# Hybrid gMLP/Mamba-2 trunk, passage to layer B: two subtractions, the time steps and a gate result moved, eight stores on another queue

## The chip, the cores and the metric

The kernel runs on one core of one Trainium2 chip. The metric is the device time of one execution in microseconds. The engines are TensorE (PE in the profile; PEld is its weight load), VectorE (DVE), ScalarE (ACT), GpSimd (POOL) and SyncE (SP), which only issues transfers. Each engine works through its own instructions in order and waits on semaphores for the others.

## The reference, cut to what matters

The trunk has two layers over 1024 tokens of width 1024. Layer A is a causal spatial gating mixer, layer B a Mamba-2 mixer. Each adds its output to the residual stream.

```python
def ssd_mixer(h, w_in, conv_w, conv_b, dt_bias, a_log, d_skip, norm_w, w_out):
    proj = h @ w_in                                   # 1024 x 1024 by 1024 x 6176
    z = proj[..., :D_INNER]                           # gate, 2048 columns
    xbc = proj[..., D_INNER:D_INNER + B_CONV_DIM]     # x, B and C, 4096 columns
    dt_raw = proj[..., D_INNER + B_CONV_DIM:]         # time steps, 32 columns
    xbc = jax.nn.silu(causal_depthwise_conv(xbc, conv_w, conv_b))
    dt = jax.nn.softplus(dt_raw + dt_bias)
    ...
    gated = (y * jax.nn.silu(z)) ...
for i in range(DEPTH):
    hn = rmsnorm(h, norm_w[i])
    h = h + mixer_i(hn)
```

What matters here is the start of layer B: `hn` is the normalised output of layer A, and the first thing computed from it is `z = hn @ w_in[:, :2048]`, with `silu(z)` kept for later, and the 32 time-step columns.

## The kernel before, in words

All large products are in float32 precision made of three passes: an operand is split into a high part (`wh`, `hh`: a cast, ScalarE, line 111) and a low part (`wl`, `hl`: source minus high part, VectorE, line 112), and `mm3` (lines 134 to 136) issues high by high, high by low and low by high. So each weight operand waits first for ScalarE and then for VectorE.

On top of this, each block of columns is computed by Strassen's scheme in Winograd's form: the activations and the weights are cut into halves both ways, and seven products replace eight. The activations' operands are `A11, A12, S4, A22, S1, S2, S3` for products 1 to 7 and are shared by all blocks; the weights' operands are `b[0,0]`, `b[1,0]`, the fourth sum (`fourth()`, line 225, `b21 - t2`), `t1`, `t2` and so on, per block. `Block.prep(n)` (line 242 on) splits the weights of product n, `Block.mm(n, i)` issues its 12 `mm3` for unit i (24 matmuls for a product of two units and 4 steps), and `Block.post(n, i)` takes a finished accumulator out of PSUM: products 1, 6 and 7 are copied to `u` by ScalarE (line 292); products 2, 5, 7 with 4, and 3 complete the quarters C11, C22, C21 and C12, and call the block's `done`. Products 6 and 7 add onto the accumulator of product 1, so product 7 must wait for the copies of product 6; product 3 adds onto that of product 5.

For the gate blocks (`z_block`, line 987 on) `done` adds the accumulator and `u` on VectorE into a tile `zt` (line 995), and `rest` applies SiLU on ScalarE (line 1000) and stores the 256 KB to `z_d` by ScalarE's queue (line 1001). The first gate block does this at once; later blocks put it off. `zt` shares a pool of four buffers (`k2`) with the time steps' `part` and the time-step weights. PSUM has six `acc` banks, three pairs of a product's two units, and two `sm` banks.

The passage from layer A to layer B is `into_b` (line 1047 on). It is written out by hand, in `manual_schedule`: each engine executes its instructions in the order in which the program names them. While the last product of layer A's output still runs, rows are normalised (`norm`, line 1059), transposed on TensorE (`tr`, line 1065) and split into operands (`first`, `second`; `both` is a cast and a subtraction, lines 1073 and 1077). `s3(tt)` (line 1103) and `s2_a(tt)` (line 1108) are VectorE subtractions that make the sums behind S3 and S2; `s2_b` splits S2 and, for every second `tt`, lets GpSimd issue an accumulating transfer for S4 (line 1114). `dt_mm(th)` computes the time steps of half the tokens into a `sm` bank, and `dt_post(th)` (lines 1037 to 1041) takes them out: a ScalarE copy, a VectorE addition, two ScalarE activations into `dtr`. The order of the first gate block is 1, 2, 4, 6, 7, 5, 3, and with the loads, `prep` and product 1 of the second block (`nxt`) behind it. `blocks` then runs the second gate block and the convolution blocks, with the decays of the time steps (`decays`, from line 1236) worked in between. The weights of the convolution blocks are summed by accumulating transfers that GpSimd issues (line 202).

Of the kernel before, what the change touches and what calls it, by code (L numbers as in the profile page):

```python
# [8 lines left out]
F32 = mybir.dt.float32  # L9
F32R = mybir.dt.float32r  # L10
AF = mybir.ActivationFunctionType
ALU = mybir.AluOpType
# [17 lines left out]
def kernel(  # L30
# [21 lines left out]
    nc = tc.nc  # L52
    x = x[0]
    out = out[0]
# [10 lines left out]
    def s8(shape, name, dt=F32):  # L65
        return sb.tile(shape, dt, name=name, tag="s8", bufs=16)
# [4 lines left out]
    def k2(shape, name, dt=F32):  # L71
        return sb.tile(shape, dt, name=name, tag="k2", bufs=4)
# [10 lines left out]
    def wh(shape):  # L83
        return sb.tile(shape, F32R, name="wh", tag="wh", bufs=3)

    def wl(shape):
        return sb.tile(shape, F32R, name="wl", tag="wl", bufs=3)
# [9 lines left out]
    def sm(name):  # L97
        return ps[0].tile([P, 512], F32, name=name, tag="sm", bufs=n_sm[0])
# [7 lines left out]
    def split(hi, lo, src, eng=None, sign=1.0):  # L106

        if sign < 0:
            nc.scalar.mul(hi, src, sign)
            return nc.vector.scalar_tensor_tensor(lo, src, sign, hi.bitcast(F32), ALU.mult, ALU.subtract)  # L110
        nc.scalar.copy(out=hi, in_=src)  # L111
        return (eng or nc.vector).tensor_tensor(out=lo, in0=src, in1=hi.bitcast(F32), op=ALU.subtract)  # L112
# [69 lines left out]
    class Block:  # L182
# [56 lines left out]
                TT(out=self.t1, in0=b[0, 1], in1=b[0, 0], op=ALU.subtract)  # L239
                TT(out=self.t2, in0=b[1, 1], in1=self.t1, op=ALU.subtract)  # L240

        def prep(self, n, lo=None):
            b = self.b
            if self.eng is not None:
                self.sum_up(n)
            src = {1: b[0, 0], 2: b[1, 0], 4: b[1, 0], 7: b[0, 1], 3: b[1, 1]}.get(n)
            if src is None:
                src = self.t1 if n == 5 else self.t2
            h_, l_ = wh([P, 4, self.cols]), wl([P, 4, self.cols])
            split(h_, l_, src, lo)  # L250
            self.Y[n] = (h_, l_)

        def sum_up(self, n):
            b, TT = self.b, self.eng.tensor_tensor
            if n in (4, 6):
                self.sums()
            if n == 4 and not self.t4:
                self.fourth()
            if n == 7:
                TT(out=b[0, 1], in0=b[1, 1], in1=b[0, 1], op=ALU.subtract)  # L260
# [291 lines left out]
    for gp in range(G // 2):  # L552
# [4 lines left out]
        if gp == 1:  # L557
# [9 lines left out]
            for h in range(2):  # L567
# [9 lines left out]
                for k in range(4):  # L577
                    g = h * 4 + k
# [25 lines left out]
    for g in range(G):  # L604
# [26 lines left out]
        def mix(m, th):  # L631
            c = g * 2 + m
            mx = sm("mx")
            for q in range(4):
# [11 lines left out]
        blk = Block(HS, lambda kh, j: [a_w_in[kh * 512:(kh + 1) * 512, j * DI + g * 256:j * DI + (g + 1) * 256]],  # L646
                    False, done_zu)
# [330 lines left out]
    z_d = [dr.tile([P, 2, T], F32, name=f"z_d{g}") for g in range(G)]  # L978
# [3 lines left out]
    def finish():  # L982

        while late:
            late.pop(0)()

    def z_block(b):

        wide = 256 if b < 3 else 128

        def done(name, i, a, u):
            th, j = 2 - int(name[1]), int(name[2]) - 1
            zt = k2([P, 512], "zt")
            if u is not None:
                nc.vector.tensor_tensor(out=zt, in0=a, in1=u, op=ALU.add)
                a = zt
            g, m = (2 * b + j, i) if b < 3 else (6, j)

            def rest():
                nc.scalar.activation(zt, a, AF.Silu)  # L1000
                nc.scalar.dma_start(out=z_d[g][:, m, th * 512:(th + 1) * 512], in_=zt)

            late.append(rest)
            if not b:
                finish()

        def W(kh, j):
            c = 512 * b + j * wide
            return [b_w_in[kh * 512:(kh + 1) * 512, c:c + wide]]

        return Block(H2, W, False, done, None, wide)

    def dt_load():


        raw = wr([P, 8, 32])
        nc.sync.dma_start(out=raw, in_=b_w_in[:, c0:c0 + 32].rearrange("(k p) n -> p k n", p=P))
        w1 = k2([P, 8, 64], "wdt", F32R)
        split(w1[:, :, 0:32], w1[:, :, 32:64], raw)
        nc.vector.tensor_tensor(out=raw[:, 4:8], in0=raw[:, 4:8], in1=raw[:, 0:4], op=ALU.subtract)  # L1020
        w0 = sb.tile([P, 4, 64], F32R, name="wdt", tag="k1", bufs=3)
        split(w0[:, :, 0:32], w0[:, :, 32:64], raw[:, 4:8])
        return [w1[:, 0:4], w0], [w1[:, 0:4], w1[:, 4:8]]

    def dt_mm(th, w):
        pd = sm("pd")
        for kh in range(2):
            X = H2[(("S1", "A22"), ("A11", "A12"))[th][kh]]
            for k in range(4):
                for x_ in X:  # L1030
                    nc.tensor.matmul(out=pd[0:64, :], lhsT=w[th][kh][:, k, :], rhs=x_[:, k, :],
                                     start=kh + k == 0 and x_ is X[0], stop=kh + k == 4 and x_ is X[1])
        return pd

    def dt_post(th, pd):
        part = k2([32, 512], "part")
        nc.scalar.copy(out=part, in_=pd[32:64, :])
        nc.vector.tensor_tensor(out=part, in0=pd[0:32, :], in1=part, op=ALU.add)
        for j in range(2):
            q = th * 2 + j  # L1040
            nc.scalar.activation(dtr[q * 32:(q + 1) * 32, :], part[:, j * 256:(j + 1) * 256], AF.Identity,
                                 bias=hv[0:32, 0:1])
# [4 lines left out]
    def into_b():  # L1047
# [4 lines left out]
        blk = zb[0]  # L1052
# [47 lines left out]
        def s3(tt):  # L1100
            if tt == 0:
                st["s3"] = s8([P, 4, 4, P], "s3")
            TTv(out=st["s3"][:, tt], in0=F[1, tt][:, 0], in1=F[0, tt][:, 0], op=ALU.subtract)

        def s2_a(tt):

            f0 = F[1, tt][:, 0]
            TTv(out=f0, in0=f0, in1=F[0, tt][:, 1], op=ALU.subtract)
# [7 lines left out]
        def both(name, tt, src):  # L1116
            hi(name, tt, src)
            lo(name, tt, src)
# [8 lines left out]
        wdt = dt_load()  # L1127
# [39 lines left out]
        pd = dt_mm(1, wdt)  # L1167
# [7 lines left out]
        blk.eng = V  # L1175
        blk.fourth()
        blk.eng = None
        blk.prep(4)
        blk.post(1, 0), blk.post(1, 1)
        s2_a(0), s3(3), s2_a(1)  # L1180
        for i in range(2):
            blk.mm(2, i, False)
        s2_b(0), s2_a(2), s2_b(1), s2_a(3), s2_b(2), s2_b(3)
        blk.prep(6)
        for tt in range(4):
            both("S3", tt, st["s3"][:, tt])
        dt_post(1, pd)
        blk.prep(7)
        for i in range(2):
            blk.mm(4, i, False)  # L1190
        for i in range(2):
            blk.mm(6, i, False)
        blk.post(6, 0), blk.post(6, 1)
        blk.post(2, 0), blk.post(2, 1)
        for i in range(2):
            blk.mm(7, i, False)
        for tt in range(4):
# [3 lines left out]
            blk.post(7, i, (0,))  # L1201
        for i in range(2):
            blk.mm(5, i, False)
        pd = dt_mm(0, wdt)
        nxt = zb[1]
        for kh, j in ((0, 0), (1, 0), (0, 1), (1, 1)):
            nxt.load(kh, j)
# [2 lines left out]
        blk.prep(3)  # L1210
        blk.post(5, 0), blk.post(5, 1)
        nxt.prep(1)
        for i in range(2):
            blk.mm(3, i, False)
        for i in range(2):
            blk.post(7, i, (1,))
        nxt.prep(2)
        for i in range(2):
            nxt.mm(1, i, False)
        dt_post(0, pd)  # L1220
        nxt.sums()
        for i in range(2):
            blk.post(3, i), nxt.post(1, i)

# [155 lines left out]
    def projections():  # L1380
# [41 lines left out]
        for kh in range(2):  # L1422
            prep(0, kh)
            yield
        last = 0
        for i, (g, kind) in enumerate(seq):
            for m in range(2):
                drain(len(queue) - last)
                ab = acc2("ab")
                for kh in range(2):  # L1430
                    for th in (1, 0):
                        for k in range(4):
                            mm3(ab[:, th, :], [w[:, k, m * P:(m + 1) * P] for w in W[i, kh]],
                                [h_[:, k, :] for h_ in H2[f"A{2 - th}{kh + 1}"]], kh == 0 and k == 0,
                                kh == 1 and k == 3)
                            if (kh, th, k) == (1, 0, 3):
                                last = push(g, kind, m, ab)
                            if k % 2:
                                yield
                    if (m, kh) == (0, 1):  # L1440
                        prep(i + 1, 0)
                    elif (m, kh) == (1, 0):
                        prep(i + 1, 1)
# [74 lines left out]
    with tc.manual_schedule():  # L1518
        into_b()
        blocks()  # L1520
# [483 lines left out]
```

## Time and profile before

| | |
|---|---|
| median of 3 runs | 1522.73 us (1522.0 to 1526.09) |
| the profiled execution: its time | 1524.54 us |
| its span | 1522.8 us |
| granted TensorE clock | 0.995 |
| TensorE busy | 97% of the span |
| VectorE, ScalarE, GpSimd busy | 69%, 51%, 26% |
| the passage, from the first transpose to the second gate block's first product | 670 to 746 us |

A row of a timeline has the start in us from the span's start, the duration in us, the engine, the line of the kernel, the operation, the tile written and those read, the shapes and a count. In brackets stands the time that the engine stood idle before it, and what ended that. A row with a count above 1 stands for several instructions in sequence. Instructions of one engine overlap a little at their edges, so the distance of starts is the cost in a row of them: 0.227 us for a matmul of 512 columns, whatever its own 0.39.

### The profile page before, as it was taken

To read this page: it belongs to the slowest core of one execution; us is meant where nothing else is said; L and a number is where in the kernel's file an instruction comes from. 1 tells how busy PE (TensorE), PEld (TensorE's weight loads), DVE (VectorE), ACT (ScalarE), POOL (GpSimd) and SP (SyncE) were. 2 spreads that over 40 slices of the span, in tenths; PEclk is the share of its full clock that TensorE was granted. 3 is DMA by queue.
4 is the path that set the end of the run, shared out by engine and by line. 5 is a ranking of instruction groups with operands and counts; after the bars stand their busy time and mean duration, and the time that the engine had idled before them with its cause. 6 is when DMAs were issued, how large, how long until landed. Compare 5 with 4: busy or idle time off the path is not lost. (4 is left out here: it accounts for less than half of the span.)

```text
span 1522.8 us, 21294 instructions
## 1 busy us (share of the span) xinstructions
PE 1477.8 (97%) x7834; PEld 1219.0 (80%) x7834; DVE 1052.6 (69%) x1712; ACT 784.2 (51%) x1257; POOL 393.3 (26%) x435
## 2 busy tenths in 40 slices
PE   6899999999999999999999999999999999999997
PEld 6899988888888888877778888877777777777875
DVE  7956566676666645678646467867677677688876
ACT  6533332322332445556656566656676666756463
POOL 1111010000000023202021223207576766642221
PEclk9999999999999999999999999999999999999999
DMA  5554323332322999947277978687666665579972
GB/s 182 140 172 141 105 89 113 105 111 93 116 96 82 351 256 239 250 130 159 97 172 153 207 152 166 139 241 208 181 153 187 160 184 139 168 250 279 258 149 111
DMA packets 175976, 254.45 MB, mean 167 GB/s; under 512 B 16400, under 2 KB 103168, under 8 KB 172672
## 3 DMA queue, kind: packets, MB, share of 16 engines
q1 hardware_dynamic: 124768, 168.93, 36.2%
q0 software_dynamic: 41168, 66.07, 22.3%
q10 hardware_dynamic: 9936, 18.09, 3.3%
q8 instruction: 62, 1.02, 0.3%
q14 instruction: 42, 0.34, 0.1%
HBM read 186.14 MB, written 51.18 MB: 156 GB/s over the span
## 5 line engine op out<-in xcount | busy, mean ns | idle before, releaser
L134 PE MATMUL acc<-hh,wh 128*128 128x512 f32 x868 | 340.9, 393 | 3.0 <-ACT wh L111 2.2
L136 PE MATMUL acc<-hh,wl 128*128 128x512 f32 x868 | 339.1, 391 | 4.3 <-DVE wl L112 4.3
L135 PE MATMUL acc<-hl,wh 128*128 128x512 f32 x868 | 338.0, 389 | 0.0
L112 DVE TENSOR_TENSOR wl<-wr,wh 128x1024 fp32r<-128x1024 f32 (+1 forms) x97 | 115.5, 1193 | 127.7 <-ACT wh L111 127.6
L136 PEld LDWEIGHTS acc<-hh,wl 128*128 128x128 f32 x868 | 162.9, 188 | 42.2 <-DVE wl L112 8.4
L134 PEld LDWEIGHTS acc<-hh,wh 128*128 128x128 f32 x868 | 163.0, 188 | 39.2 <-ACT wh L111 4.3
L135 PEld LDWEIGHTS acc<-hl,wh 128*128 128x128 f32 x868 | 163.1, 188 | 32.9
L292 ACT COPY u<-acc 128x512 f32<-128x512 f32 x115 | 66.7, 582 | 193.4 <-PE acc L136 192.1
L111 ACT CAST wh<-wr 128x1024 fp32r<-128x1024 f32 (+1 forms) x113 | 116.3, 1030 | 95.4 <-PE acc L135 56.7
L136 PE MATMUL acc<-wh,hl 128*128 128x256 f32 x448 | 128.6, 287 | 4.9 <-DVE hl L403 3.5
L134 PE MATMUL acc<-wh,hh 128*128 128x256 f32 x448 | 129.0, 288 | 3.4 <-DVE wh L414 1.4
L134 PE MATMUL ab<-hh,wh 128*128 128x512 f32 x288 | 128.2, 445 | 2.1 <-DVE x L1305 1.1
L135 PE MATMUL acc<-wl,hh 128*128 128x256 f32 x448 | 128.1, 286 | 1.3 <-DVE wl L417 1.3
L136 PE MATMUL ab<-hh,wl 128*128 128x512 f32 x288 | 113.4, 394 | 0.0
L135 PE MATMUL ab<-hl,wh 128*128 128x512 f32 x288 | 112.3, 390 | 0.0
L136 PEld LDWEIGHTS acc<-wh,hl 128*128 128x128 f32 x448 | 87.2, 195 | 6.0 <-DVE hl L403 4.2
L134 PEld LDWEIGHTS acc<-wh,hh 128*128 128x128 f32 x448 | 87.1, 195 | 4.3 <-ACT hh L396 1.6
L135 PEld LDWEIGHTS acc<-wl,hh 128*128 128x128 f32 x448 | 87.2, 195 | 1.7 <-DVE wl L417 1.5
L1582 ACT ACTIVATE wl<-wl,tk 128x128 f32<-128x128 f32 x256 | 81.6, 392 | 1.3 <-DMA wl<-cs_d 1.0
L135 PE MATMUL bo<-wl,xh 128*128 128x512 f32 x192 | 76.4, 398 | 3.6 <-DVE wl L738 1.8
L645 POOL DMA_DIRECT2D y_d<-y x8 | 4.4, 548 | 290.9 <-DVE y L642 290.9
L112 DVE TENSOR_TENSOR wl<-t,wh 128x1024 fp32r<-128x1024 f32 (+1 forms) x38 | 45.4, 1196 | 48.9 <-ACT wh L111 48.7
(312 smaller groups left out, 3243.2 us busy)
## 6 DMA issues: line engine op xcount, KB each, us to landing
wr<-in_a_w_in_dram SPq DMA_DIRECT2D x48, 512.0 KB, 3.7
wl<-cs_d SPq DMA_DIRECT2D x64, 256.0 KB, 3.4
wr<-in_b_w_in_dram SPq DMA_DIRECT2D x30, 512.0 KB, 7.1
wb<-in_a_w_out_dram SPq DMA_DIRECT2D x10, 1024.0 KB, 12.2
wb<-in_b_w_out_dram SPq DMA_DIRECT2D x10, 1024.0 KB, 11.4
wr<-in_b_w_in_dram SPq DMA_DIRECT2D x36, 256.0 KB, 7.1
v<-v_d SPq DMA_DIRECT2D x8, 1024.0 KB, 4.8
y_d<-y POOLq DMA_DIRECT2D x8, 1024.0 KB, 5.8
```

What stands on the lines that cost most here:

```text
L111: nc.scalar.copy(out=hi, in_=src)
L112: return (eng or nc.vector).tensor_tensor(out=lo, in0=src, in1=hi.bitcast(F32), op=ALU.subtract)
L134: nc.tensor.matmul(out=o, lhsT=l[0], rhs=r[0], start=start, stop=False, **kw)
L135: nc.tensor.matmul(out=o, lhsT=l[0], rhs=r[1], start=False, stop=False, **kw)
L136: nc.tensor.matmul(out=o, lhsT=l[1], rhs=r[0], start=False, stop=stop, **kw)
L292: nc.scalar.copy(out=self.u[n][:, i], in_=a)
L645: store = lambda: nc.gpsimd.dma_start(out=y_d[-1], in_=y)
L1582: nc.scalar.activation(wl[:, j, :], wl[:, j, :], AF.Relu, scale=-1.0, bias=tokc(2, c, self.g)[:, j:j + 1])
```

## The change

Four edits in the passage:

- In `prep`, the low part of the weights can be put into a list and issued later. For the fourth weights, VectorE now issues `s2_a(0)` and `s3(3)` between ScalarE's cast and that low part. They stood behind `post(1, 0)` and `post(1, 1)` before.
- `dt_post(1, pd)` goes from behind the split of S3 to behind product 3. The second half's bank gets a name of its own, `pd0`, since both are now held at once, and `dt_post(0, pd0)` goes behind the second block's `sums()`.
- `post(2, 0)` and `post(2, 1)`, the first gate quarter C11, go from ahead of product 7 to ahead of product 3 and behind the second block's `prep(1)`.
- The stores of the first gate block are issued by GpSimd instead of ScalarE.

```diff
-        def prep(self, n, lo=None):
+        def prep(self, n, lo=None, rest=None):
...
             h_, l_ = wh([P, 4, self.cols]), wl([P, 4, self.cols])
-            split(h_, l_, src, lo)
             self.Y[n] = (h_, l_)
+            if rest is None:
+                split(h_, l_, src, lo)
+            else:
+                nc.scalar.copy(out=h_, in_=src)
+                rest.append(lambda: nc.vector.tensor_tensor(out=l_, in0=src, in1=h_.bitcast(F32), op=ALU.subtract))
...
                 nc.scalar.activation(zt, a, AF.Silu)
-                nc.scalar.dma_start(out=z_d[g][:, m, th * 512:(th + 1) * 512], in_=zt)
+                (nc.scalar if b else nc.gpsimd).dma_start(out=z_d[g][:, m, th * 512:(th + 1) * 512], in_=zt)
...
         blk.eng = None
-        blk.prep(4)
+        low = []
+        blk.prep(4, rest=low)
+        s2_a(0), s3(3)
+        low.pop()()
         blk.post(1, 0), blk.post(1, 1)
-        s2_a(0), s3(3), s2_a(1)
+        s2_a(1)
...
             both("S3", tt, st["s3"][:, tt])
-        dt_post(1, pd)
         blk.prep(7)
...
         blk.post(6, 0), blk.post(6, 1)
-        blk.post(2, 0), blk.post(2, 1)
         for i in range(2):
             blk.mm(7, i, False)
...
             blk.mm(5, i, False)
-        pd = dt_mm(0, wdt)
+        pd0 = dt_mm(0, wdt)
...
         nxt.prep(1)
+        blk.post(2, 0), blk.post(2, 1)
         for i in range(2):
             blk.mm(3, i, False)
+        dt_post(1, pd)
         for i in range(2):
             blk.post(7, i, (1,))
         nxt.prep(2)
         for i in range(2):
             nxt.mm(1, i, False)
-        dt_post(0, pd)
         nxt.sums()
+        dt_post(0, pd0)
         for i in range(2):
             blk.post(3, i), nxt.post(1, i)
```

## The prediction, on record before the result

> **What bounds the kernel now.** I read the page first, then TensorE's timeline in the passage to layer B, then VectorE's and ScalarE's timelines there, then the stalls behind the passage, last the DMA issues.
>
> ```profile
> span 1522.8 us, 21294 instructions
> PE 1477.8 (97%) x7834; PEld 1219.0 (80%) x7834; DVE 1052.6 (69%) x1712; ACT 784.2 (51%) x1257; POOL 393.3 (26%) x435
> ```
>
> TensorE sets the time. A change that removes no matmul can gain only where TensorE stands still. TensorE's timeline in the passage (start, duration, then idle time and releaser): the first matmul of product 4, the five stalls, and the first matmul of two consecutive products:
>
> ```profile
> 711.02 0.39 PE L134 MATMUL acc<-hh,wh 128*128 128x512 f32 x1
> ...
> 717.34 0.50 PE L134 MATMUL acc<-hh,wh 128*128 128x512 f32 x1 [0.53 <-ACT wh L111]
> 718.60 0.50 PE L136 MATMUL acc<-hh,wl 128*128 128x512 f32 x1 [0.53 <-DVE wl L112]
> 724.34 0.50 PE L134 MATMUL acc<-hh,wh 128*128 128x512 f32 x1 [0.46 <-ACT u L292]
> 730.88 0.50 PE L134 MATMUL acc<-hh,wh 128*128 128x512 f32 x1 [0.61 <-ACT wh L111]
> 732.13 0.50 PE L136 MATMUL acc<-hh,wl 128*128 128x512 f32 x1 [0.52 <-DVE wl L112]
> ...
> 740.93 0.40 PE L134 MATMUL acc<-hh,wh 128*128 128x512 f32 x1
> 746.39 0.39 PE L134 MATMUL acc<-hh,wh 128*128 128x512 f32 x1
> ```
>
> An undisturbed product of 24 matmuls takes 746.39 - 740.93 = 5.46 us, 0.227 per matmul. Stalls stand ahead of product 6 (717.34, 718.60), 7 (724.34) and 5 (730.88, 732.13). Each costs its idle figure and about 0.25 of restart: 718.60 comes 1.26 after 717.34 where two matmuls take 0.45, so it lost 0.8. Together the five lost about 4 us. That is all that this passage has to give.
>
> **Fourth weights and subtractions.** VectorE (L112 at 717.31 makes product 6's low part):
>
> ```profile
> 707.91 1.22 DVE L225 TENSOR_TENSOR wr<-wr,t 128x1024 f32<-128x1024 f32 x1
> 710.24 1.23 DVE L112 TENSOR_TENSOR wl<-wr,wh 128x1024 fp32r<-128x1024 f32 x1 [1.11 <-ACT wh L111]
> ...
> 711.98 0.68 DVE L1103 TENSOR_TENSOR s<-f,nrm 128x512 f32<-128x512 f32 x1
> 712.59 0.69 DVE L1108 TENSOR_TENSOR f<-f,nrm 128x512 f32<-128x512 f32 x1
> ...
> 717.31 1.23 DVE L112 TENSOR_TENSOR wl<-t,wh 128x1024 fp32r<-128x1024 f32 x1 [0.24 <-ACT wh L111]
> 718.46 2.49 DVE L1077 TENSOR_TENSOR hl<-s,hh 128x512 fp32r<-128x512 f32 x4
> 720.86 0.67 DVE L1038 TENSOR_TENSOR part<-pd,part 32x512 f32<-32x512 f32 x1
> ```
>
> After L225 VectorE idles 1.11 us for ScalarE's cast. The subtractions s2_a(0) and s3(3) take 0.61 each (712.59 - 711.98), 1.2 in all: they fill the hole from 709.05 and the low part starts at 710.26 instead of 710.24, so the fourth product loses at most 0.02. s2_a(1), at 712.59 now, starts at 711.4. ScalarE's casts of S2 follow VectorE's subtractions and VectorE's low parts follow those, so the interleaved chain up to product 6's weights moves by 1.2. ScalarE then casts product 6's weights by 716.1, ahead of 716.6 when TensorE has done product 4 (711.02 + 5.46 and a short wait), and the low part ends at 717.35 instead of 718.54: product 6's third matmul starts at 717.4. **Gain 1.2**; 0.3 of wait is left.
>
> **Time steps later.** ScalarE:
>
> ```profile
> 717.19 2.18 ACT L1073 CAST hh<-s 128x512 fp32r<-128x512 f32 x4
> 719.39 0.58 ACT L1037 COPY part<-pd 32x512 f32<-32x512 f32 x1
> 721.57 1.03 ACT L1041 ACTIVATE dtr<-part,hv 32x256 f32<-32x256 f32 x2 [1.60 <-DVE part L1038]
> 722.63 1.05 ACT L111 CAST wh<-wr 128x1024 fp32r<-128x1024 f32 x1
> 723.70 1.08 ACT L292 COPY u<-acc 128x512 f32<-128x512 f32 x2
> ...
> 726.60 0.63 ACT L1000 ACTIVATE zt<-zt 128x512 f32<-128x512 f32 x1 [0.40 <-ACT zt L1000]
> ...
> 727.69 2.18 ACT L1073 CAST hh<-nrm 128x512 fp32r<-128x512 f32 x4 [0.45 <-ACT zt L1000]
> ```
>
> dt_post holds ScalarE from 719.39 to 722.6, 3.2 us, half of it waiting for VectorE. The copies of product 6 (723.70) queue behind it, and product 7, which adds onto the same banks, waits for them at 724.34. Without dt_post product 7's weights are cast by 719.2, the first copy follows product 6's first half at about 720, and product 7 starts as product 6 ends. **Gain 0.6 and 0.2** of restart.
>
> **First gate's result later.** Row by row between those copies and S1's casts (727.69):
>
> ```profile
> 724.85 1.28 DVE L995 TENSOR_TENSOR zt<-acc,u 128x512 f32<-128x512 f32 x2
> 725.57 0.63 ACT L1000 ACTIVATE zt<-zt 128x512 f32<-128x512 f32 x1 [0.79 <-DVE zt L995]
> 726.23 0.33 ACTq L1001 DMA_DIRECT2D z_d<-zt  x1
> ```
>
> Two additions, two activations and two stores hold ScalarE until 727.69. Without them S1's casts start when product 6's second half is copied, at 723.2, product 5's weights are cast by 726.4 and their low part ends at 727.6; TensorE is free for product 5 at 728.0. Both stalls (730.88, 732.13; 0.61 and 0.52, each with 0.25 of restart) go, **gain 1.6**. post(2) holds two PSUM banks longer, so product 5 must take those of product 1, copied out by ScalarE at 726.3 to 726.9: 1.1 us to spare. If that cover fails, product 5 waits for as long as the copy is late. The POOL transfers of S4 start 1.2 earlier and are due only at 728.7.
>
> TensorE so stands 1.2 + 0.8 + 1.6 = 3.6 us earlier at product 5.
>
> **What is late next.** The moved work lands ahead of the second gate block.
>
> ```profile
> 731.68 2.19 ACT L1073 CAST hh<-f 128x512 fp32r<-128x512 f32 x4
> 737.45 0.69 DVE L995 TENSOR_TENSOR zt<-acc,u 128x512 f32<-128x512 f32 x1 [0.78 <-PE acc L136]
> 753.17 1.05 ACT L111 CAST wh<-t 128x1024 fp32r<-128x1024 f32 x1
> 762.11 0.59 ACT L292 COPY u<-acc 128x512 f32<-128x512 f32 x1 [0.40 <-ACT zt L1000]
> 762.75 0.50 PE L134 MATMUL acc<-hh,wh 128*128 128x512 f32 x1
> 769.27 0.50 PE L136 MATMUL acc<-hh,wl 128*128 128x512 f32 x1 [0.33 <-DVE wl L112]
> ```
>
> S4's casts start at 728.7 (after product 7's second copy, which waits for TensorE at 728.2), 3.0 before 731.68. From there to 753.17 ScalarE and VectorE work almost without a pause. Added there: two activations (1.26) and dt_post (0.58 + 0.67 + 1.03), 3.5 in all. Taken away: six store turns of 0.40 (the idle time in row 726.60), 2.4, and the 0.78 at 737.45, since that half is done early. Net +0.4: the cast at 753.17 comes 3.0 - 0.4 = 2.6 earlier, still in time for the second block's product 6. But its product 7 (762.75) starts now right as the copy of 762.11 ends (762.70). TensorE, 3.6 early, waits there 1.0 for a ScalarE that is 2.6 early. The next stall, 769.27, hangs on the same chain (VectorE's time-step formula ahead of L112) and moves by 2.6 too. **1.0 of the 3.6 is given back.**
>
> **Stores by GpSimd.**
>
> ```profile
> v_d<-vt POOLq DMA_DIRECT2D x24, 256.0 KB, 2.7
> z_d<-zt ACTq DMA_DIRECT2D x28, 256.0 KB, 4.3
> L337 POOL DMA_DIRECT2D v_d<-vt x24: 540/540/583, 84.2 to 199.2; - x24
> 774.02 1.29 POOL L202 DMA_DIRECT2D t<-in_b_w_in_dram  x1 [56.85 <-ACT wr L212]
> DMA to landing us min/median/max: 2.4/4.3/7.8
> ```
>
> The eight stores (the last row is z_d's landing) go to an engine that idles 56.85 us before 774.02. The nearest row is v_d<-vt: the same 256 KB on the same queue, 0.54 on GpSimd and 2.7 to landing. I take 2.7; the ends are 2.4 and 7.8. GpSimd's work costs nothing: the next on its queue is the addition at 774. Landings matter through the buffers: zt and part share four, one of them held by the time-step weights until dt_mm(0) ends (737.1). By my sum the second C21 result, due at 740.7, reuses the buffer stored at 738.4: it needs a landing within 2.3 us, so 2.7 makes a wait of 0.4, inside the 2.6.
>
> By the Trainium skill's page "SBUF — State Buffer" (section "SBUF: two separate sides") this move is a trap: a GpSimd-issued DMA may have to wait for VectorE to release a shared port before its descriptors can be written, 620 ns growing to 3100 in its example; ScalarE's queue is free of that. If each landing grew by that 2.5, as an estimate from the page, hardly any gain would be left. The 24 v_d rows, at 540 to 583 ns, do not show it.
>
> **Sum.** 3.6 - 1.0 = 2.6. The profiled execution took 1524.54 (span 1522.8 and 1.7 around it), so 1521.9 by it; the median 1522.73 lies 1.8 below that execution, so I forecast 1520.1. About 0.3% (4.6 us) is what a measurement of this kernel can tell from no change.
>
> **Rivals.**
>
> *The zt buffers block (slower).* From a landing of 2.7 on, each further us holds VectorE at the second C21 result, and with it the second block's weights and the formula ahead of 769.27. At 5.3 the gain is gone; at 7.8, the longest landing that z_d's rows show, the kernel is 2.5 slower, 1525.2. For it: the change sends the stores from one queue to another in a stretch where buffers turn round faster. Against: v_d's 2.7. The skill's rule on the shared port would act through this. 0.10, of which beyond no gain 0.05.
>
> *A transfer decides (no gain).*
>
> ```profile
> 798.55 1.05 ACT L111 CAST wh<-t 128x1024 fp32r<-128x1024 f32 x1 [6.54 <-DMA t<-in_b_w_in_dram]
> 799.65 0.50 PE L134 MATMUL acc<-hh,wh 128*128 128x512 f32 x1 [0.79 <-ACT wh L111]
> ```
>
> The conv block's sums land at 798.5 and TensorE waits for them. If that landing stayed, TensorE would lose here whatever it had won: 1522.7. For it: GpSimd's queue is dense from 774 on. Against: its first addition is released by ScalarE (row 774.02), which moves by 2.6. 0.15.
>
> *The second block keeps up (full gain).* If the copy of 762.11 and the chain behind it come earlier than I sum, up to 3.6 stays: 1519.1. 0.10.
>
> *It does not do what it says:* if the subtractions ended after the cast, the hole would only change its owner; 0.02 by rows, so I give it nothing of its own.
>
> **Numbers.** Forecast 0.65, rivals 0.10, 0.15, 0.10. From full gain less 1 us of run spread (1518) to no gain with the spread above (1524.2, a part of the slower rival in it). Faster by over 0.3% needs full gain and luck of a run: 0.10; slower 0.04, a late landing; the rest within, 0.86.
>
> **What would show it.** Right: VectorE without the 1.11 before L112 at 710; no stall ahead of products 7 and 5; about 0.3 left ahead of product 6; mm(3) some 3.6 earlier; a wait of about 1 us ahead of the second block's product 7, on ScalarE's copy; the conv block's cast on t about 2.6 earlier. Wrong: VectorE waiting for a landing of z_d before an L995; product 5 released by ScalarE's copy of u; the cast at 798.5 unmoved; or POOL stores far above 0.54.

## The result, and the profile after

The kernel after took 1519.58 us (median of 6 runs, 1518.95 to 1522.92); the kernel before, beside it, 1524.62 (6 runs, 1522.0 to 1526.88). The ratio is 0.9974, with a 95% interval of 0.9964 to 0.9984: about 4.0 us faster, from 2.4 to 5.5 (the two medians lie 5.0 apart, and the runs of each kernel 4 to 5). The gain is within the 0.3% bound of the prediction and the time inside its range, but 4.0 is more than the 2.6 us of its sum. The profiled execution took 1518.95 us, its span is shown here, with the busy time of the engines:

```profile
span 1517.2 us, 21301 instructions
PE 1475.4 (97%) x7834; PEld 1220.2 (80%) x7834; DVE 1052.5 (69%) x1712; ACT 783.6 (52%) x1257; POOL 397.6 (26%) x443
```

The span is 5.6 us shorter. Part of that isn't the change's. These are the last transposes of the passage in TensorE's timelines, of before and then of after; no instruction ahead of them was changed:

```profile
704.48 1.23 PE L1065 MATMUL tp<-ident,nrm 128*128 128x128 f32 x8
```

```profile
703.38 1.23 PE L1069 MATMUL tp<-ident,nrm 128*128 128x128 f32 x8
```

They stand 1.10 earlier already; in the other runs below, with the same instructions ahead of them, they start at 702.68 to 705.34. So times are compared from this row on ("earlier" means this from now on). From here to the end of the span before needs 1522.8 - 704.48 = 818.3 us and after 1517.2 - 703.38 = 813.8: **4.5 us earlier**, beside 4.0 by the ratio.

**In the passage the forecast holds.** VectorE after:

```profile
706.81 1.22 DVE L225 TENSOR_TENSOR wr<-wr,t 128x1024 f32<-128x1024 f32 x1
707.94 0.69 DVE L1112 TENSOR_TENSOR f<-f,nrm 128x512 f32<-128x512 f32 x1
708.55 0.69 DVE L1107 TENSOR_TENSOR s<-f,nrm 128x512 f32<-128x512 f32 x1
709.15 1.23 DVE L255 TENSOR_TENSOR wl<-wr,wh 128x1024 fp32r<-128x1024 f32 x1
...
715.03 1.23 DVE L112 TENSOR_TENSOR wl<-t,wh 128x1024 fp32r<-128x1024 f32 x1 [0.25 <-ACT wh L111]
```

The hole of 1.11 is filled, and product 6's low part starts 1.2 earlier (715.03 - 703.38 = 11.65; before 717.31 - 704.48 = 12.83). TensorE after, product 6's third matmul, the first ones of products 7 and 5, and product 7 of the second block:

```profile
716.31 0.50 PE L136 MATMUL acc<-hh,wl 128*128 128x512 f32 x1
...
721.45 0.39 PE L134 MATMUL acc<-hh,wh 128*128 128x512 f32 x1
...
726.89 0.39 PE L134 MATMUL acc<-hh,wh 128*128 128x512 f32 x1
...
759.55 0.50 PE L134 MATMUL acc<-hh,wh 128*128 128x512 f32 x1 [1.60 <-ACT u L296]
```

Only about 0.3 is left ahead of product 6's third matmul; a row without brackets ahead of products 7 and 5 means that nobody was waited for. Then, as forecast, ScalarE's copy is late for the second block's product 7: 1.60 of idle time, 1.76 with the restart. ScalarE after:

```profile
727.57 2.18 ACT L1077 CAST hh<-f 128x512 fp32r<-128x512 f32 x4
...
746.72 1.03 ACT L1045 ACTIVATE dtr<-part,hv 32x256 f32<-32x256 f32 x2 [3.80 <-DVE part L1042]
...
749.91 1.06 ACT L111 CAST wh<-t 128x1024 fp32r<-128x1024 f32 x1
...
758.91 0.58 ACT L296 COPY u<-acc 128x512 f32<-128x512 f32 x1 [0.45 <-ACT zt L1004]
```

S4's casts start 3.0 earlier (24.19 behind the transposes, before 27.20), which is the forecast; the cast for the second block's product 6 only 2.16 (46.53, before 48.69), where 2.6 was forecast.

**Behind it something happens that the sum did not have.** The stores (a group of one line's instructions), their landing (2.4 us by the median of the eight), and the one wait for a buffer (VectorE's timeline):

```profile
L1005 POOL DMA_DIRECT2D z_d<-zt x8: 540/540/611, 733.5 to 749.8; - x8
```

```profile
z_d<-zt POOLq DMA_DIRECT2D x8, 256.0 KB, 2.4
```

```profile
740.04 0.69 DVE L999 TENSOR_TENSOR zt<-acc,u 128x512 f32<-128x512 f32 x1 [0.18 <-DMA z_d<-zt]
```

These are as forecast. But now the sums of the conv block. Before, ScalarE's first instruction for them; after, the same, GpSimd's first transfer and ScalarE's cast:

```profile
771.74 1.04 ACT L211 ACTIVATE t<-wr 128x1024 f32<-128x1024 f32 x1
```

```profile
768.48 1.04 ACT L211 ACTIVATE t<-wr 128x1024 f32<-128x1024 f32 x1
769.83 1.32 POOL L202 DMA_DIRECT2D t<-in_b_w_in_dram  x1 [19.44 <-ACT t L211]
792.09 1.05 ACT L111 CAST wh<-t 128x1024 fp32r<-128x1024 f32 x1 [3.32 <-DMA t<-in_b_w_in_dram]
```

L211 is 2.16 earlier, with the chain. The first accumulating transfer follows it by 1.35, where before it followed by 2.28 (774.02 - 771.74); and the cast, which waits for the last of them, follows L211 by 23.6 where before it was 26.8 (798.55 - 771.74). So the cast is 5.4 earlier than before, not 2.6, and TensorE no longer waits for it (before 0.79, then 0.53 for the low part, about 1.9 with the restarts, by the starts of the matmuls on both sides). The landings of the four transfers of these sums, before and then after:

```profile
DMA to landing us min/median/max: 6.1/14.7/18.2
```

```profile
DMA to landing us min/median/max: 6.0/10.7/16.0
```

The ledger of the trace, by the starts of the same matmuls: TensorE is 2.10 earlier at the second block's product 7 (759.55 - 703.38 = 56.17; before 762.75 - 704.48 = 58.27), 2.25 earlier ahead of the conv block's product, 4.1 behind its first matmuls, 4.6 behind 880 us and 4.0 again at 1380 us. There the trace of before, on TensorE, has this wait:

```profile
1384.28 0.50 PE L135 MATMUL bo<-wl,xh 128*128 128x512 f32 x1 [1.81 <-DVE wl L738]
```

Behind it matmuls follow each other by 0.43 us for about 3.4 us, which costs 1.6; the trace of after has the wait (1.79) and not the slow matmuls, and loses 1.1 in small waits behind it. That is no effect of the change: the kernel before, profiled once more, has the same wait (1.80) without them. So 4.0 of the 4.5 are left for the change, and the rest lies in these two executions.

### The profile page after: what moved, and what is told of

It is laid out like the page before. It is cut to its first block, busy times and chain, and to the rows that moved or that the text cites. A ratio compares the mean times of both kernels' runs of the same rounds, so it can differ in the third digit from the quotient of the medians.

```text
span 1517.2 us, 21301 instructions
## 1 busy us (share of the span) xinstructions
PE 1475.4 (97%) x7834; PEld 1220.2 (80%) x7834; DVE 1052.5 (69%) x1712; ACT 783.6 (52%) x1257; POOL 397.6 (26%) x443
## 4 chain that ended last, share of the span: by engine, by line
PE 63%; issue 14%; DVE 10%; DMA 5%; ACT 5%; POOL 2%; SPq 0%; ACTq 0%; POOLq 0%; DVEq 0%
PE acc L136 9%; PE acc L134 9%; PE acc L135 9%; PE ab L134 4%; PE ab L136 4%; PE ab L135 4%; PE ao L136 3%; PE ao L135 3%; PE ao L134 3%; PE yy L1616 2%; PE yy L1620 2%; DMA t<-in_b_w_in_dram 2%; DVE wl L112 2%; PE sp L1627 2%; PE bo L135 1%
```

## The experiments

The question: which of the four edits carries the measured gain, and why do the conv block's sums land 3.2 earlier after L211? Theory: the eight stores on GpSimd's queue let GpSimd send the first accumulating transfer earlier, and that decides the landing. Rivals: the landing is chance; the gain is that of the passage; GpSimd was slow only because it, or its queue, had paused for 57 us.

All ratios are against the kernel before, run beside it, with 95% intervals. The last three columns are from the profiled execution: first transfer behind the start of L211, the conv block's cast behind the start of L211, and TensorE's idle time ahead of the conv block's product (high part, low part). With the decays later that cast waited for no transfer.

| kernel | ratio | transfer | cast | idle |
|---|---|---|---|---|
| before, again | 1.0006 (0.9996 to 1.0017) | 2.28 | 26.9 | 0.89, 0.53 |
| after, stores by ScalarE | 1.0011 (1.0002 to 1.0019) | 2.29 | 26.7 | 0.67, 0.53 |
| before, subtractions only | 0.9986 (0.9977 to 0.9995) | 2.29 | 27.3 | 1.14, 0.53 |
| before, one GpSimd copy added | 1.0002 (0.9993 to 1.0010) | 2.28 | 26.8 | 0.81, 0.53 |
| before, one store by GpSimd | 0.9997 (0.9988 to 1.0006) | 2.29 | 27.1 | 0.77, 0.53 |
| before, stores only | 0.9973 (0.9963 to 0.9983) | 1.34 | 23.7 | none |
| before, subtractions and stores | 0.9965 (0.9953 to 0.9977) | 1.34 | 23.7 | none |
| after | 0.9974 (0.9964 to 0.9984) | 1.35 | 23.6 | none |
| after, decays later | 0.9978 (0.9968 to 0.9989) | 1.37 | 25.5 | none |
| after, first gate result back | 0.9963 (0.9950 to 0.9975) | 1.34 | 24.1 | none |
| after, first transfer held | 0.9985 (0.9977 to 0.9994) | 2.73 | 27.2 | 0.90, 0.53 |

**The kernel before, once more** (no edit).

> The kernel before, unchanged, for a second profile. The two theories differ on the conv block's cast on t, which waited 6.54 us for a transfer in the first profile, with TensorE 0.79 idle behind it. Theory (the transfer comes earlier because the whole chain ahead of it does): this profile looks like the first one, the cast 27.8 us after the first L211 ACTIVATE of the second block's sums (771.74 and 798.55 there), the stall there again. Rival (the transfer's length changes from one execution to the next and the change has nothing to do with it): that distance differs by over 1 us from the first profile's. Ratio 1.000 in both, within 0.1%.

The 27.8 is a slip: 798.55 - 771.74 is 26.8.

ScalarE's cast in this run:

```profile
798.30 1.04 ACT L111 CAST wh<-t 128x1024 fp32r<-128x1024 f32 x1 [6.64 <-DMA t<-in_b_w_in_dram]
```

It stands 26.9 behind L211, against 26.8 in the first trace. Chance falls as an explanation.

**The kernel after, all stores by ScalarE again.**

```diff
-                (nc.scalar if b else nc.gpsimd).dma_start(out=z_d[g][:, m, th * 512:(th + 1) * 512], in_=zt)
+                nc.scalar.dma_start(out=z_d[g][:, m, th * 512:(th + 1) * 512], in_=zt)
```

> The changed kernel with the first gate block's eight stores on ScalarE's queue again. Theory (the second block's product 7 waits for ScalarE's chain): six store turns of 0.40 come back on that chain, so the cast of the second block's product 6 comes about 2.4 us later and the stall ahead of product 7 grows from 1.8 to about 4; the stalls in the passage stay away; about 2 us slower than the changed kernel, 0.998 to 0.999 of the kernel before. Rival (the moved result and time steps bring the gain, the store queue is hidden): stall ahead of product 7 unchanged at 1.8, 0.997.

The three edits of order by themselves are not faster: 1.0011. The passage's stalls are gone as in the kernel after, but ScalarE, with its store turns back, is late for the second block's product 6. TensorE's timeline, and below it the stretch of 756 to 762 us by engine (time, PE, PEld, DVE, ACT, POOL, granted clock, DMA share, GB/s):

```profile
756.59 0.50 PE L134 MATMUL acc<-hh,wh 128*128 128x512 f32 x1 [2.16 <-ACT wh L111]
...
757.86 0.50 PE L136 MATMUL acc<-hh,wl 128*128 128x512 f32 x1 [0.53 <-DVE wl L112]
...
759.03 0.63 PE L134 MATMUL acc<-hh,wh 128*128 128x512 f32 x1
759.45 0.63 PE L135 MATMUL acc<-hl,wh 128*128 128x512 f32 x1
```

```profile
756.00:762.00 6.00, 4.88 (x13) 3.56 (x14) 4.43 (x5) 3.20 (x4) 0.00 (x0) 0.73 0.03 10
```

The wait takes 2.16 and 0.53, and behind it eight matmuls follow each other by 0.43 instead of 0.227, another 1.6 us, while the granted clock of the stretch is 0.73. Won in the passage, lost ahead of the next block, in this execution with interest.

**The kernel before with the stores alone** (the same line, in the other direction).

> The kernel before with nothing but the eight stores by GpSimd. Theory: two store turns leave the passage ahead of S1's casts, so the stalls ahead of product 5 start 0.8 earlier, and six leave ScalarE's chain behind it, so that the second block's stalls (769.27, 774.86, 776.12 before) shrink; 1 to 2 us faster, 0.999. Rival (the stores alone decide the transfer at the conv block, since GpSimd's queue is then awake): the first accumulating transfer follows L211 by 0.3 us instead of 1.2, the conv cast no longer stalls TensorE, and 2 us or more are gained with the passage's stalls as they were.

0.9973: as much as all four edits together, though in the passage only the first of product 5's two stalls is gone and TensorE waits ahead of products 6 and 7 as it did before. GpSimd and ScalarE:

```profile
771.55 1.32 POOL L202 DMA_DIRECT2D t<-in_b_w_in_dram  x1 [21.03 <-ACT t L211]
```

```profile
793.95 1.05 ACT L111 CAST wh<-t 128x1024 fp32r<-128x1024 f32 x1 [3.44 <-DMA t<-in_b_w_in_dram]
```

L211 starts at 770.21: 1.34 to the transfer, 23.7 to the cast, no stall at the conv block. By the starts of TensorE's matmuls, 1.0 is won at product 5, another 0.7 at the second block, as the theory has it for the free store turns, and 1.9 at the conv block, as the rival has it. Both hold, and each is about half.

**The kernel before with the subtractions alone.**

```diff
-        blk.prep(4)
+        low = []
+        blk.prep(4, rest=low)
+        s2_a(0), s3(3)
+        low.pop()()
         blk.post(1, 0), blk.post(1, 1)
-        s2_a(0), s3(3), s2_a(1)
+        s2_a(1)
```

> The kernel before with nothing but the two subtractions in VectorE's wait. Theory: product 6 starts 1.2 earlier and all that follows on ScalarE and VectorE with it, so the stalls ahead of 7 and 5 stay as long as they were and 1.2 us is kept up to the conv block: 0.999. Rival (the hole is filled for nothing, ScalarE's copies of product 6 set product 7): the stall ahead of product 7 grows by what product 6 wins, 1.000.

Product 6 comes 1.2 earlier, and the ratio of 0.9986 (2.1 us, 0.8 to 3.5) agrees with a gain of that size. The 1.2 stand up to the conv block. There the wait is longer in the profiled execution, and what follows it is slow, so that nothing is left of them behind it:

```profile
797.67 0.50 PE L134 MATMUL acc<-hh,wh 128*128 128x512 f32 x1 [1.14 <-ACT wh L111]
...
798.93 0.65 PE L136 MATMUL acc<-hh,wl 128*128 128x512 f32 x1 [0.53 <-DVE wl L112]
```

```profile
798.00:803.00 5.00, 4.47 (x13) 3.23 (x12) 3.30 (x4) 2.53 (x5) 1.35 (x1) 0.66 0.24 32
```

Again matmuls at 0.43 behind the wait, with a granted clock of 0.66. Whether the other executions pay that too no trace shows.

**A GpSimd instruction ahead of the sums.** Does GpSimd answer late because it has idled for 57 us? The kernel before, with one copy of a column that nobody uses, 18 us ahead of L211.

```diff
+        Gp.tensor_copy(out=tiny([P, 8], "poke")[:, 0:1], in_=nxt.u[1][:, 1, 0:1])
```

> The kernel before, its stores on ScalarE's queue, with one added GpSimd instruction: a copy of one column of the second block's u, which can run at about 753, 20 us ahead of the first accumulating transfer of the second block's sums. Its result is not used. Theory (GpSimd answers late after 57 us without work, and the eight stores shorten that pause): the first transfer starts 1.35 us after L211 instead of 2.28, the conv block's cast comes 23.7 us after L211 instead of 26.8, its stalls (1.8 us with the restart) go, and so may the next one at 877; the stalls of the passage stay; 1.8 to 3 us faster, 0.998 to 0.9988. Rival (the transfers come earlier because stores have left ScalarE's queue, or because GpSimd's transfer queue itself must have been in use): 2.28 and 26.8 as before, 1.000.

```profile
772.97 1.29 POOL L202 DMA_DIRECT2D t<-in_b_w_in_dram  x1 [20.40 <-ACT wr L212]
```

L211 starts at 770.69: still 2.28, though GpSimd idled for 20 us only, as in the kernel after. Its own pause is not the cause.

**One store by GpSimd**, the last of the eight. Is it the pause of its transfer queue?

```diff
-                nc.scalar.dma_start(out=z_d[g][:, m, th * 512:(th + 1) * 512], in_=zt)
+                q = nc.gpsimd if not b and name == "C12" and i == 1 else nc.scalar
+                q.dma_start(out=z_d[g][:, m, th * 512:(th + 1) * 512], in_=zt)
```

> The kernel before with only the last of the eight stores (C12, second unit) by GpSimd, some 20 us ahead of the first accumulating transfer of the second block's sums. Theory (the first transfer that GpSimd issues after some 57 us without a transfer goes out 0.95 us late, and that is why the conv block's cast waits; an instruction that is no transfer does not help, as the copy of one column showed): first transfer 1.35 us after L211 begins instead of 2.28, the conv cast 23.7 us after L211 instead of 26.8, TensorE's stalls there gone while those of the passage stay; 1.5 to 3 us faster, 0.998 to 0.999. Rival (the eight stores together do it, by the place of the later transfers among GpSimd's instructions or by ScalarE's shorter chain): 2.28 and 26.8 as before, 0.9997 to 1.000.

```profile
772.05 1.28 POOL L202 DMA_DIRECT2D t<-in_b_w_in_dram  x1 [20.31 <-ACT wr L212]
```

L211 starts at 769.76: 2.29, and no gain (0.9997). That theory falls too.

**The first transfer held back.** The kernel after, with five copies of one column on GpSimd between L211 and the first transfer; their results aren't used.

```diff
+            if self.hold:
+                t = tiny([P, 8], "hold")
+                for _ in range(5):
+                    nc.gpsimd.tensor_copy(out=t[:, 0:1], in_=self.t2[:, 0, 0:1])
             self.add(self.t2, 0, 0)
...
+        bs[1].hold = True
```

> The changed kernel with five copies of one column by GpSimd, each about 0.2 us, between L211 and the first accumulating transfer of the second block's sums, so that this transfer goes out about 1 us later, as it does in the kernel before. Theory (that one microsecond decides the landing): the conv cast comes about 26.8 us after L211 begins instead of 23.6, TensorE stalls there again by 1.8 with the restart, 2 us or more slower than the changed kernel, about 0.9985 to 0.999 of the kernel before. Rival (the landing follows from what else is under way, not from the start of the first transfer): the cast moves by 1 us at most, no stall, 0.997.

GpSimd, ScalarE, TensorE, and the landings of the four transfers:

```profile
769.34 1.16 POOL L216 COPY hold<-t 128x1 f32<-128x1 f32 x5 [19.29 <-ACT t L211]
770.88 1.31 POOL L202 DMA_DIRECT2D t<-in_b_w_in_dram  x1 [0.37 <-POOL hold L216]
```

```profile
795.36 1.04 ACT L111 CAST wh<-t 128x1024 fp32r<-128x1024 f32 x1 [6.75 <-DMA t<-in_b_w_in_dram]
```

```profile
796.45 0.50 PE L134 MATMUL acc<-hh,wh 128*128 128x512 f32 x1 [0.90 <-ACT wh L111]
```

```profile
DMA to landing us min/median/max: 5.9/14.0/18.3
```

With L211 at 768.15 the transfer goes out 2.73 behind it, 1.4 later than in the kernel after, and the cast comes 27.2 behind it, 3.6 later; the landings are those of the kernel before, the conv block's stall is back, and of the gain of 0.0026 there is 0.0015 left (the two intervals overlap a little; the trace does not leave it open). So it is the time at which the transfers go out that sets the landing, and not the stores as such.

The copies hold back the second of the four transfers too, and in the traces it is the second that pays. Its row on GpSimd, before and then after; below them SyncE's load of weights, before:

```profile
774.79 1.81 POOL L202 DMA_DIRECT2D wr<-in_b_w_in_dram  x1
```

```profile
770.92 1.53 POOL L202 DMA_DIRECT2D wr<-in_b_w_in_dram  x1
```

```profile
776.09 0.37 SPq L120 DMA_DIRECT2D wr<-in_b_w_in_dram  x1
```

Counted from the start of L211, the second transfer's row ends at 4.9 before, 5.3 in the held kernel and 4.0 after; SyncE's load goes out at 4.4 in all three. The DMA queues from 7.5 to 9.5 us behind L211 (packets, MB, share of the engines; q0 carries GpSimd's transfers, q1 SyncE's), before and then after:

```profile
q1 hardware_dynamic: 433, 0.44, 86.9%
q0 software_dynamic: 30, 0.02, 5.9%
```

```profile
q0 software_dynamic: 233, 0.24, 75.0%
q1 hardware_dynamic: 220, 0.23, 41.3%
```

Before, SyncE's load has this stretch nearly to itself, and the second transfer lands 12.8 us after it went out; after, the two share it, and it lands after 9.1. In the held kernel it is 0.09 MB on q0 against 0.45 on q1, and 12.0. The other kernels divide in the same way, but for the one with the decays later: there SyncE's load goes out only at 8.01, and the second transfer lands after 7.8. So the landing fits a race: a second transfer that comes in behind SyncE's load has to let it pass. No run moved that load by itself; this is read from the traces and was not tried.

**The decays later.** The kernel after, with the time steps' formulas of the second block let in two units, that is one product, later, to free ScalarE and VectorE ahead of its product 7.

```diff
-            if not done and next(small, 0) == 0:
+            if not done and turn[0] > 2 and next(small, 0) == 0:
```

> The changed kernel with the time steps' formula begun two units later in the second gate block. Theory (what the passage gains is given back because ScalarE's table loads and VectorE's formula stand ahead of the second block's products 7, 5 and 4): the copy of product 6 comes ahead of 757.8, the 1.76 ahead of product 7 goes, and most of the 0.42 + 0.47 + 0.70 behind it; up to 3.5 us faster than the changed kernel, 0.995 to 0.9965 of the kernel before. Rival (the formula only moves the waits, to product 5 or 3, or the conv block's transfer decides): a stall of the same size turns up later, 0.997 to 0.998.

```profile
761.80 0.50 PE L134 MATMUL acc<-hh,wh 128*128 128x512 f32 x1 [1.44 <-ACT u L296]
```

The wait only moves by one unit, to the second half of product 7. 0.9978, no gain on the kernel after.

**The time steps back, and the first gate's result back**, each alone on the kernel after.

```diff
+        dt_post(1, pd)
         blk.prep(7)
...
-        dt_post(1, pd)
```

> The changed kernel with the second half's time steps taken out where they were, behind S3's split. Theory: ScalarE is held 3.2 us (less the store turns, which do not touch it) there, so product 7 waits again for the copies of product 6, by 0.5 to 0.9, while the second block's cast for product 6 comes about 2 earlier than in the changed kernel and the stall ahead of its product 7 shrinks to nearly nothing: the passage's loss is made good. Rival: the stall ahead of the second block's product 7 stays at 1.8.

```diff
+        blk.post(2, 0), blk.post(2, 1)
         for i in range(2):
             blk.mm(7, i, False)
...
-        blk.post(2, 0), blk.post(2, 1)
```

> The changed kernel with the first gate's C11 result where it was, ahead of product 7. Theory: S1's casts come later by two additions and activations, about 2.1 us, with the POOL stores no store turns; product 5 waits again, by 0.5 to 1.3 in all, and the stall ahead of the second block's product 7 shrinks by as much or more, since ScalarE has that work done early. Rival: product 5 does not wait, because the stores were what held ScalarE.

> The changed kernel with the first gate's C11 result where it was before, timed. Theory (with the stores on GpSimd, ScalarE has room for it in the passage, and later it only lengthens the chain to the second block): no stall ahead of the second block's product 7, 1 to 2 us faster than the changed kernel, 0.996 to 0.997 of the kernel before. Rival (a gain in one profile only): 0.9975.

With the time steps back, product 7 waits for ScalarE's copy again, but the wait ahead of the second block's product 7 is gone (one execution, 1517.64 us):

```profile
721.34 0.50 PE L134 MATMUL acc<-hh,wh 128*128 128x512 f32 x1 [0.42 <-ACT u L296]
```

With the gate's result back, the passage waits 0.30 ahead of product 6's low part, much as the kernel after does, and 0.28 ahead of product 5's, and the second block's product 7 doesn't wait either: 1518.12 us in the single execution, then 0.9963 when timed. That is the lowest ratio of all, though its interval overlaps that of the kernel after.

**Subtractions and stores** on the kernel before; the time steps of the second half and the gate's result stay where they were, those of the first half go behind the second block's sums.

```diff
             both("S3", tt, st["s3"][:, tt])
+        dt_post(1, pd)
...
+        blk.post(2, 0), blk.post(2, 1)
         for i in range(2):
             blk.mm(7, i, False)
```

(This is written against the kernel after; the two calls are taken out further down.)

> The kernel before with the subtractions in VectorE's wait and the stores by GpSimd; the C11 result and the second half's time steps stay where they were, only the first half's time steps come after the second block's sums. Theory: ScalarE is held in the passage, so products 7 and 5 wait (0.6, and 0.5 to 1.3), and the second block finds ScalarE early, with no stall ahead of its product 7; the sum is that of the changed kernel or better, 0.996 to 0.9975. Rival (the moved result and time steps carry the gain): 0.998 or more.

```profile
723.87 0.50 PE L134 MATMUL acc<-hh,wh 128*128 128x512 f32 x1 [0.46 <-ACT u L296]
...
730.67 0.50 PE L136 MATMUL acc<-hh,wl 128*128 128x512 f32 x1 [0.41 <-DVE wl L112]
```

Two stalls of the passage are back, none stands ahead of the second block's product 7, and the ratio is 0.9965: no worse than with all four edits.

## Why the prediction was right, and where it was off

- **Fourth weights and subtractions** (1.2): right. 1.19 at product 6's third matmul (12.93 behind the transposes; before 14.12), about 0.3 left.
- **Time steps later** (0.6 and 0.2) and **first gate's result later** (1.6): right in their place, the three stalls are gone. By the end of product 6 of the second block TensorE is 2.10 + 1.76 = 3.86 earlier; the sum said 3.6.
- **What is late next** (1.0 given back, 2.6 left): right in mechanism and place, too small. 1.76 is given back and 2.10 is left. The term that was off is ScalarE's and VectorE's chain between S4's casts and the second block's cast: it starts 3.0 earlier as forecast, but loses 0.85 instead of 0.4. The 2.4 that the store turns free on ScalarE is not all progress, for ScalarE there waits 3.80 for VectorE's addition of the moved time steps (row 746.72). So the two later moves, worth 2.4 in the passage, are mostly lost again. It fits this that putting either of them back cost no time in the runs made, and that subtractions and stores give 0.9965 without them.
- **Stores by GpSimd**, costed at nothing beyond the store turns: this is the step that failed. As to itself it was right: 0.54 us each, landing 2.4 by the median where 2.7 was taken, a wait of 0.18 for a buffer where 0.4 was forecast, and the rival in which the buffers block did not come. The rule of the Trainium skill's page "SBUF — State Buffer" that was weighed there (section "SBUF: two separate sides") would have shown, as an estimate from that page's figures, as stores or landings some 2.5 us longer; VectorE was at work for 9.98 of the 17 us in which they were issued (below, time, PE, PEld and then DVE), and 540 to 611 ns and the 2.4 speak against it for its operations here. But the stores have an effect of their own, further on: 1.9 at the conv block, about half of what they alone give (0.9973).

```profile
733.00:750.00 17.00, 17.00 (x76) 13.39 (x75) 9.98 (x13) 10.42 (x19) 4.04 (x8) 1.00 0.49 160
```

- **A transfer decides** was the rival with the right place and the wrong sign. I held the conv block's landing to move with the chain or to stay. It moves by more: the chain's 2.16, and 3.2 because the transfers follow L211 sooner. That this is cause and not company is shown by the held transfer, where the landing goes back with it.

That the forecast of 1520.1 was so close to the median of 1519.58 is luck. It was 2.6 below a median of 1522.73, and the kernel before took 1524.62 beside the kernel after, 1.9 more. As to the change itself, less was kept in the passage than the sum said (2.10, not 2.6), and 1.9 came from a stall that it left in place.

**What stays open** is why GpSimd sends that transfer 0.95 late without the eight stores. The late answer is the odd one. In the same trace of before, the same transfer of a later block (ScalarE, then GpSimd):

```profile
886.64 1.06 ACT L211 ACTIVATE t<-wr 128x1024 f32<-128x1024 f32 x1
```

```profile
887.99 1.28 POOL L202 DMA_DIRECT2D t<-in_b_w_in_dram  x1 [6.89 <-ACT t L211]
```

It follows the end of L211 by 0.29, as in the kernel after (0.31), while the first one of before, and that of the five late kernels of the table that hold nothing back, follows it by 1.24 or 1.25. In the program the late ones have one semaphore more to wait for ahead of this transfer, that of S4's last transfer (four instead of three), for which one of the eight stores has waited already. This goes with the late start in every run, but it is not shown as its cause: the transfer at 887.99 has six to wait for and is not late, and S4's last transfer went out 58 us earlier. Neither GpSimd's own pause nor that of its queue is it (the copy and the single store). The wait by itself was not tried. The brackets of the late rows name L212 as what ended the wait, those of the early rows L211, and the late ones start 0.14 or 0.15 us behind the end of L212 (before at 773.87) in every trace. But in the programs of both kernels the transfer waits for the count that L211 sets, and the other releases by ScalarE above take about 0.3; so whether L212 has a part in it stays open too.

## What to carry to other kernels

A stall taken from one stage is kept only as far as the chain of the next stage comes earlier too; here ScalarE and VectorE, not TensorE, said what of 3.86 us was left at the second block. When an edit touches a queue, look at what goes through that queue next, and how much later its answers land: here the first of several transfers, about 1 us sooner, was worth more than two moves of compute, most likely because the next one came in ahead of another queue's load. And take a change of several edits apart: one line of four, by itself, measured as much as all four.

## What the runs showed of the hardware that was not expected

- **A wait can be dearer than its length, and not in every execution.** Behind idle times of 2.16 and 0.53 us, and of 1.14 and 0.53, TensorE's matmuls followed each other by 0.43 us instead of 0.227 for about 3.4 us, with granted clocks of 0.73 and 0.66 in those stretches: 1.6 us on top. Behind the 1.60 in the kernel after, the 0.90 and 0.53 of the held transfer and the 0.79 and 0.53 of before it did not happen. Behind one and the same wait of the kernel before, near 1384 us, it happened in one execution (1.81) and not in the other (1.80), so the length alone doesn't decide. The Trainium skill's page "TensorE: Matmul & The Clock Gate" (section "What's actually happening") has the clock halved after an idle window of about 3.4 us that runs freely; the halved pace and its 3.4 us agree, but here idle times of 1.7 to 2.7 in all, in one piece or cut in two by a pair of matmuls, were enough. The page's advice to avoid gaps over about 3 us (section "Why this matters for your kernels") is too lenient for this kernel.
- **A landing hangs steeply on the issue.** With the first of four accumulating transfers 0.95 to 1.4 us later, the cast that waits for the last of them came 26.7 to 27.3 us behind L211 instead of 23.6 to 24.1, in every run in which it waited for them. The step lies in the second of the four: it lands 12.0 to 12.8 us after it went out where its row ends behind the issue of SyncE's load, and 9.1 to 9.4 where it ends ahead of it.
